# A trunk of attention and feed-forward layers: other banks for two accumulators of the last attention branch, and turns and value products grouped by unit

## Chip, core and metric

The kernel runs on one core of one Trainium2 chip. The metric is the device time of one execution in microseconds (us). It was run three times: median 1346.76 us, lowest 1345.96, highest 1348.61.

## What is computed

Two layers (DEPTH = 2) work on 256 positions of 1024 features. Each layer is a half-weighted SwiGLU feed-forward, an attention block with three branches, a second feed-forward, and a gated projection:

```python
for i in range(DEPTH):
    h = h + 0.5 * swiglu(rms_norm(h, norm_g[i, 0]), ffn1_wi[i], ffn1_wo[i])
    n = rms_norm(h, norm_g[i, 1])
    ... = split_cols(n @ w_in[i], IN_SPLITS)
    ya = diff_attention(...)      # branch a: 4 heads of two score maps
    yb = nsa_attention(...)       # branch b: compressed + selected + window keys, 8 heads in 2 groups
    yc = swa_sink_attention(...)  # branch c: window of 128 and a sink
    merged = (sigmoid(ga) * (ya @ w_branch[i, 0]) + sigmoid(gb) * (yb @ w_branch[i, 1])
              + sigmoid(gc) * (yc @ w_branch[i, 2]))
    h = h + merged @ w_out[i]
    h = h + 0.5 * swiglu(rms_norm(h, norm_g[i, 2]), ffn2_wi[i], ffn2_wo[i])
    h = h + sigmoid(rms_norm(h, norm_g[i, 3]) @ w_ple_gate[i]) * (p[i] @ w_ple[i])
return rms_norm(h, final_norm)
```

All of it is float32. The kernel splits each operand into a high and a low part and forms a product as three matmuls, high times high, high times low, low times high (`mul3`, lines 235 to 237).

## The kernel before

The 256 positions are two tiles, t = 0 and t = 1, of 128. Weights come in pieces of 128x1024 (`raw`), which ScalarE copies to a high part `wh` (line 228) and VectorE subtracts to a low part `wl` (line 223). Six pieces fit (`WBUFS`), so a piece can be written when an older one has been read by both tiles. A product of 8 steps runs tile 0 first and tile 1 eight steps behind it.

Attention work is written as generators that advance by a step after some matmuls of the projections ("`flow.tick`"). A scheduler then orders the instructions of each engine by its own model of their times, so the order in the code is not the order on an engine.

Branch b has six units, called B1 to B6 here: B1 and B2 are tile 0 of key groups 0 and 1 with both key sets, B3 and B4 tile 1 of group 0 with the selected and the window keys, B5 and B6 the same of group 1. `first` of a unit makes the scores (`s`, line 537) and the softmax: VectorE's line 546, ScalarE's exponentials (line 548), and VectorE's scalings of `p`. `second` turns the weights `p` on TensorE four blocks at a time (`pt`, line 243), splits each turn into high and low `pT` (ScalarE line 228, then VectorE line 223; three buffers), and adds two products of 512 columns for each turn to `yb` (`weighted`, lines 790 and 791). Each of B1 to B6 has two turns. After B1, B2, B4 and B6 a compressed part (`own`, `pcT`) is added to `yb`, and `gather` moves `yb` to `yt` (ScalarE lines 796 and 797, VectorE line 800) and splits it to `yB`, which `br` reads.

PSUM (the accumulators that TensorE writes) has eight banks in named rings: `mm` 2, `s` 2, `tp` 3 (all transposes), `y` 1. So B5's first product into `yb` has to wait until `gather` of B4 has read the one `y` bank.

The last branch, b, ends so: both gate products, then `tile(0)`, then `tile(1)`: the two halves (c = 0, 1) of `br` for that tile, each mixed into `merged` by VectorE (lines 970 and 971), transposed (`mt`, line 243) and split to `mT` (lines 231 and 232). Then come the two halves of the product with `w_out` (`wo`). `wo` of tile 0 needs `mT` of tile 0 only; `wo` of tile 1 needs the end of `tile(1)`.

The `product` function takes its banks from `mm`, and where `wide[0]` is set two of every four from `s`:

```python
    def product_bank(name):

        wide[1] += 1
        return bank("s" if wide[0] and wide[1] % 4 >= 2 else "mm", 2, name)
```

Of the kernel before, what the change touches and what calls it, by code (L numbers as in the profile page):

```python
# [186 lines left out]
def trunk(ctx: ExitStack, tc: tile.TileContext, a: dict, out: bass.AP, index: list):  # L187
# [14 lines left out]
    wide = [True, 0]  # L202
# [9 lines left out]
    def y_bank(name):  # L212
        return bank("y", 1, name)
# [290 lines left out]
    def attention(i, norm, after):  # L504
# [76 lines left out]
        qk, va, yA = [None] * 2, [None], [None] * NT  # L581
# [16 lines left out]
        def attend_a():  # L598
            bnd = band(0)

            def first(u):
                m, t = u
                nk = 128 * (t + 1)
                s = scores("s", qk[m], [0, 1], t, lambda x, r, k: qk[m][r, x, 2 + k, :nk])
                yield
                p = pool.tile([128, 4, 256], F32, tag="p", bufs=3, name="p")
                st = None
                for st in softmax([p[:, j, :nk] for j in range(4)], [s[j // 2][:, j % 2, :nk] for j in range(4)],
                                  [back(bnd[:, 2 * m + j % 2], nk) for j in range(4)]):
                    yield  # L610
                nc.vector.reciprocal(st[:, 8:12], st[:, 4:8])
                nc.vector.tensor_scalar(st[:, 10:12], st[:, 10:12], nlam[:, i:i + 1], None, op0=ALU.mult)
                for x in range(2):
                    nc.vector.tensor_scalar(p[:, 2 + x, :nk], p[:, 2 + x, :nk], st[:, 10 + x:11 + x], None, op0=ALU.mult)
                    nc.vector.scalar_tensor_tensor(p[:, x, :nk], p[:, x, :nk], st[:, 8 + x:9 + x], p[:, 2 + x, :nk],
                                                   op0=ALU.mult, op1=ALU.add)
                yield
                return p

            def second(u, p):  # L620
                m, t = u
                T = []
                for k in range(t + 1):
                    T.append(turned([p[:, x, k * 128:(k + 1) * 128] for x in range(2)]))
                    yield
                y_ps = y_bank("ya")[:, :256]
                for x in range(2):
                    o, hd = slice(x * 128, x * 128 + 128), slice((2 * m + x) * 128, (2 * m + x + 1) * 128)
                    for k in range(t + 1):
                        mul3(y_ps[:, o], T[k][:, 0, x, :], T[k][:, 1, x, :], va[0][:, 0, k, hd], va[0][:, 1, k, hd], k == 0, k == t)  # L630
                    yield
                y = pool.tile([128, 256], F32, tag="yt", bufs=2, name="yn")
                st = pool.tile([128, 32], F32, tag="st", bufs=4, name="st")
                for x in range(2):
                    o = slice(x * 128, x * 128 + 128)
                    nc.scalar.activation(y[:, o], y_ps[:, o], AF.Square, accum_out=st[:, x:x + 1])
                nc.vector.tensor_scalar(st[:, 2:4], st[:, 0:2], 1.0 / 128, EPS, op0=ALU.mult, op1=ALU.add)
                nc.gpsimd.tensor_tensor(st[:, 4:6], st[:, 2:4], mhalf[:, :2], op=ALU.pow)
                nc.vector.tensor_tensor(y.rearrange("p (h e) -> p h e", h=2), y_ps.rearrange("p (h e) -> p h e", h=2),
                                        st[:, 4:6, None].to_broadcast([128, 2, 128]), op=ALU.mult)  # L640
                yield
                if m == 0:
                    yA[t] = y_tile("yA")
                ps = tp_bank("yt")
                transposes(ps, [y[:, x * 128:x * 128 + 128] for x in range(2)])
                split(yA[t][:, 0, 2 * m:2 * m + 2], yA[t][:, 1, 2 * m:2 * m + 2],
                      ps[:, :256].rearrange("p (k q) -> p k q", k=2), sg[:, i:i + 1])
                yield

            yield from pipelined([(m, t) for m in range(2) for t in range(NT)], first, second)  # L650


# [189 lines left out]
        def attend_b():  # L842
            bnd, y_ps = {}, {}

            def first(u):
                g, t, ss = u
                if g not in bnd:
                    bnd[g] = band(4 + 4 * g)
                if t == 0:
                    p = pool.tile([128, 4, 2, 128], F32, tag="p", bufs=3, name="p")  # L850
                    s = scores("s", qB[0], [2 * g, 2 * g + 1], 0, lambda x, r, m: kB[0][r, x, g:g + 3:2, :128])
                    rows = [(j, k) for j in range(4) for k in range(2)]
                    pr = [p[:, j, k] for j, k in rows]
                    sr = [s[j // 2].rearrange("p m (k n) -> p m k n", k=2)[:, j % 2, k] for j, k in rows]
                    br = [back(bnd[g][:, j], 128) for j, k in rows]
                else:
                    p = pool.tile([128, 4, 256], F32, tag="p", bufs=3, name="p")
                    s = scores("s", qB[0], [2 * g, 2 * g + 1], 1, lambda x, r, m: kB[0][r, x, 2 * ss[0] + g, :])
                    pr = [p[:, j] for j in range(4)]
                    sr = [s[j // 2][:, j % 2] for j in range(4)]  # L860
                    br = [back(bnd[g][:, j], 256) for j in range(4)]
                n = len(pr)
                yield
                st = None
                for st in softmax(pr, sr, br):
                    yield
                nc.vector.reciprocal(st[:, 2 * n:3 * n], st[:, n:2 * n])
                for k, x in enumerate(ss):
                    o = st[:, 2 * n + k:3 * n:len(ss)]
                    nc.vector.tensor_tensor(o, o, sig[t][:, 8 + 8 * x + 4 * g:12 + 8 * x + 4 * g], op=ALU.mult)  # L870
                for j in range(n):
                    nc.vector.tensor_scalar(pr[j], pr[j], st[:, 2 * n + j:2 * n + j + 1], None, op0=ALU.mult)
                yield
                return p

            def second(u, p):
                g, t, ss = u
                if yB[t] is None:
                    yB[t] = y_tile("yB")
                if ss[0] == 0:  # L880
                    y_ps[g, t] = y_bank("yb")
                for x in ss:
                    for k in range(t + 1):
                        T = turned([p[:, j, x, :] if t == 0 else p[:, j, 128 * k:128 * k + 128] for j in range(4)])
                        yield
                        weighted(y_ps[g, t], vB[0][:, x, k, g], T.rearrange("p x j q -> p x (j q)"), x == 0 and k == 0, False)
                        yield
                if ss[-1] == 1:
                    while t not in pcT:
                        yield  # L890
                    T = own(t, g)
                    yield
                    weighted(y_ps[g, t], vc[0][:, 0], T.rearrange("p x j q -> p x (j q)"), False, True)
                    gather(yB[t], y_ps[g, t], g)
                    readyB[t] += 1
                    yield

            yield from pipelined([(g, t, ss) for t, sets in ((0, [(0, 1)]), (1, [(0,), (1,)])) for g in range(2) for ss in sets], first, second)
# [16 lines left out]
        def attend_c():  # L915
# [26 lines left out]
            def second(u, p):  # L942
                g, t = u
                y_ps = y_bank("yc")
                for k in range(t + 1):
                    T = turned([p[:, j, 128 * k:128 * k + 128] for j in range(4)])
                    yield
                    weighted(y_ps, vC[0][:, k, g], T.rearrange("p x j q -> p x (j q)"), k == 0, k == t)
                    yield
                gather(yC[t], y_ps, g)  # L950
                yield
# [4 lines left out]
        def branch(b, yT, side, last=False):  # L956
# [32 lines left out]
            if last:  # L989
# [3 lines left out]

                def tile(t):
                    for c in range(2):
                        ps = product_bank(f"br{t}")
                        for k in range(4):
                            wh, wl = ws[c](k)
                            mul3(ps, yT[t][:, 0, k, :], yT[t][:, 1, k, :], wh, wl, k == 0, k == 3)
                            flow.tick()  # L1000
                        with tc.high_priority(offset=150):
                            both[c][1](t, ps)
# [40 lines left out]
        yield lambda: start("compressed", compressed(), 1.0, 1)  # L1043
        yield from branch(2, yC, "c")
        yield from branch(1, yB, "b", True)
        yield lambda: wide.__setitem__(0, True)
        for c in range(2):
            yield product(lambda t, k: (mT[t][:, 0, k, :], mT[t][:, 1, k, :]), NK, after(c), "wo", streamed(i, f"wo{c}", 512))

# [197 lines left out]
```

## Time and profile before

| what | value |
|---|---|
| median of 3 runs | 1346.76 us |
| the profiled execution | 1346.13 us, of which the span in the profile is 1344.3 us |
| granted TensorE clock, mean | 0.999 |
| busy: TensorE matmul, weight load, VectorE, ScalarE | 99%, 81%, 70%, 58% |
| attention of layer 0, of layer 1 | about 196 to 462 us, about 860 to 1126 us |

A busy share is that of the whole span. Matmuls overlap in the profile: a row's duration is longer than the distance to the next row's start, and the distance is what a matmul costs.

### The profile page before, as it was taken

What the parts mean: (1) busy time and instruction counts of PE and PEld (TensorE: products, weight loads), DVE (VectorE), ACT (ScalarE), POOL (GpSimd) and SP (SyncE); (2) the same over time, 40 slices, a digit from 0 to 9 for tenths busy, and PEclk for the clock granted to TensorE, in tenths of its full rate; (3) what the DMA queues carried; (4) which work ended last, traced back from release to release, by engine and by line L of the source; (5) the groups of instructions that cost most, each with busy time, mean ns of one, the idle gap of its engine ahead of it and who ended that gap; (6) DMA issues with size and microseconds to landing.
All of it is one profiled execution on the core that took longest, in us unless ns stands there. A gap on an engine that the chain in (4) does not pass through costs nothing.

```text
span 1344.3 us, 18242 instructions
## 1 busy us (share of the span) xinstructions
PE 1326.3 (99%) x6414; PEld 1093.2 (81%) x6414; DVE 945.9 (70%) x1795; ACT 783.0 (58%) x1382; POOL 20.4 (2%) x36
## 2 busy tenths in 40 slices
PE   9999999999999999999999999999999999999997
PEld 7778888887887788888888888888888878888886
DVE  6677566768978767665776766577697886767565
ACT  7555455668756555544755545566696656555454
POOL 0000000000000000000000000000000000000000
PEclk9999999999999999999999999999999999999999
DMA  8887665455742578675567875744556425877562
GB/s 302 214 270 220 206 207 187 141 165 168 229 153 79 188 186 237 208 219 184 188 199 216 224 209 186 243 152 162 167 174 207 152 78 177 242 222 214 189 209 78
DMA packets 121993, 257.14 MB, mean 191 GB/s; under 512 B 56944, under 2 KB 62500, under 8 KB 121902
## 3 DMA queue, kind: packets, MB, share of 16 engines
q1 hardware_dynamic: 121150, 254.34, 61.1%
q0 software_dynamic: 320, 1.08, 0.3%
q8 instruction: 50, 0.82, 0.3%
q10 hardware_dynamic: 432, 0.56, 0.1%
q14 instruction: 41, 0.34, 0.1%
HBM read 243.33 MB, written 1.08 MB: 182 GB/s over the span
## 4 chain that ended last, share of the span: by engine, by line
PE 91%; DVE 4%; DMA 2%; ACT 1%; issue 1%; SPq 0%; POOLq 0%; POOL 0%; DVEq 0%; ACTq 0%
PE ff L236 11%; PE ff L237 11%; PE ff L235 11%; PE fo L235 6%; PE fo L236 6%; PE fo L237 6%; PE gate L235 3%; PE gate L237 3%; PE gate L236 3%; PE s L537 2%; PE A L235 2%; PE A L236 2%; PE A L237 2%; DVE wl L223 2%; PE br L236 1%; PE br L235 1%
## 5 line engine op out<-in xcount | busy, mean ns | idle before, releaser
L223 DVE TENSOR_TENSOR wl<-raw,wh 128x1024 fp32r<-128x1024 f32 (+1 forms) x448 | 539.4, 1213 | 174.2 <-ACT wh L228 166.8
L228 ACT ACTIVATE wh<-raw 128x1024 fp32r<-128x1024 f32 (+1 forms) x448 | 468.3, 1050 | 229.0 <-PE fo L237 85.4
L236 PE MATMUL ff<-wl,nT 128*128 128x512 f32 x704 | 273.8, 391 | 1.6 <-DVE wl L223 1.5
L237 PE MATMUL ff<-wh,nT 128*128 128x512 f32 x704 | 272.8, 390 | 0.0
L235 PE MATMUL ff<-wh,nT 128*128 128x512 f32 x704 | 270.9, 391 | 0.3 <-ACT wh L228 0.3
L236 PEld LDWEIGHTS ff<-wl,nT 128*128 128x128 f32 x704 | 132.3, 188 | 30.9 <-DVE wl L223 3.9
L235 PEld LDWEIGHTS ff<-wh,nT 128*128 128x128 f32 x704 | 132.3, 188 | 29.5 <-ACT wh L228 2.1
L237 PEld LDWEIGHTS ff<-wh,nT 128*128 128x128 f32 x704 | 132.3, 188 | 27.3
L236 PE MATMUL fo<-wl,gT 128*128 128x512 f32 x352 | 134.2, 392 | 0.0
L237 PE MATMUL fo<-wh,gT 128*128 128x512 f32 x352 | 133.7, 389 | 0.0
L235 PE MATMUL fo<-wh,gT 128*128 128x512 f32 x352 | 132.5, 389 | 0.0
L474 ACT ACTIVATE act<-ff,stats 128x256 f32<-128x256 f32 x88 | 41.4, 472 | 85.9 <-PE ff L237 85.7
L475 DVE TENSOR_TENSOR gated<-act,ff 128x256 f32<-128x256 f32 x88 | 36.6, 417 | 60.1 <-ACT act L474 60.1
L235 PEld LDWEIGHTS fo<-wh,gT 128*128 128x128 f32 x352 | 66.1, 188 | 13.8
L237 PEld LDWEIGHTS fo<-wh,gT 128*128 128x128 f32 x352 | 66.1, 188 | 13.4
L236 PEld LDWEIGHTS fo<-wl,gT 128*128 128x128 f32 x352 | 66.1, 188 | 13.3
L235 PE MATMUL gate<-wh,nT 128*128 128x512 f32 x192 | 76.3, 399 | 0.0
L237 PE MATMUL gate<-wh,nT 128*128 128x512 f32 x192 | 76.1, 396 | 0.0
L236 PE MATMUL gate<-wl,nT 128*128 128x512 f32 x192 | 75.9, 395 | 0.0
L228 ACT ACTIVATE gT<-whole 128x512 fp32r<-128x512 f32 (+1 forms) x48 | 28.4, 591 | 64.3 <-DVE whole L448 64.2
L548 ACT ACTIVATE p<-p,st 128x128 f32<-128x128 f32 (+1 forms) x128 | 56.8, 445 | 2.9 <-DVE st L546 2.2
L448 DVE COPY whole<-flip 128x512 uint16<-128x512 uint16 (+1 forms) x96 | 38.2, 433 | 14.5 <-DMA flip<-cut 13.9
(301 smaller groups left out, 1997.6 us busy)
## 6 DMA issues: line engine op xcount, KB each, us to landing
raw<-in_wst SPq DMA_DIRECT2D x438, 512.0 KB, 4.4
band<-table SPq DMA_DIRECT2D x10, 512.0 KB, 5.1
raw<-in_wbv SPq DMA_DIRECT2D x4, 420.0 KB, 3.0
flip<-cut SPq DMA_TRANSPOSE x96, 4.1
xt<-in_xt SPq DMA_DIRECT2D x4, 256.0 KB, 5.3
raw<-in_wst SPq DMA_DIRECT2D x4, 256.0 KB, 4.9
h<-in_x SPq DMA_DIRECT2D x2, 512.0 KB, 7.6
band<-table POOLq DMA_DIRECT2D x2, 512.0 KB, 6.9
```

The lines of the kernel that those rows point to most:

```text
L223: nc.vector.tensor_tensor(o, x, y, op=ALU.subtract)
L228: nc.scalar.activation(hi, src, AF.Copy)
L235: nc.tensor.matmul(ps, xh, wh, start=start, stop=False)
L236: nc.tensor.matmul(ps, xh, wl, start=False, stop=False)
L237: nc.tensor.matmul(ps, xl, wh, start=False, stop=stop)
L448: tc.keep_in_program_order(nc.vector.tensor_copy(halves(whole)[:, :128 * m, w], flip[:, w, :m].rearrange("p a b -> p (a b)")))
L474: nc.scalar.activation(act, ps[:, :256], AF.Silu, scale=norm.r(t))
L475: nc.vector.tensor_tensor(held[t][:, 256 * (f % 2):256 * (f % 2) + 256], act, ps[:, 256:], op=ALU.mult)
L537: nc.tensor.matmul(o, q[r, x, qb[m], t * 128:(t + 1) * 128], kk, start=x + y == 0, stop=x == 1)
L548: nc.scalar.activation(p[j], p[j], AF.Exp, bias=st[:, j:j + 1], scale=-1.0, accum_out=st[:, n + j:n + j + 1])
```

## The change

1. Branch a: a unit's two turns become one run of four transposes with one split of 128x512.
2. Branches b and c: all turns of a unit stand ahead of its value products in the code.
3. `yb` of B5 and B6 is taken from the ring `s`, whose last scores are those of B6.
4. The first half of `tile(1)`'s `br` is taken from `s` too; the other three stay in `mm`.
5. At the end of the branch the counter `wide[1]` is set to -1, so that both tiles of the first `wo` half use `mm` and both of the second `s`.

```diff
-                T = []
-                for k in range(t + 1):
-                    T.append(turned([p[:, x, k * 128:(k + 1) * 128] for x in range(2)]))
-                    yield
+                T = turned([p[:, x, k * 128:(k + 1) * 128] for k in range(t + 1) for x in range(2)])
+                yield
...
-                    y_ps[g, t] = y_bank("yb")
-                for x in ss:
-                    for k in range(t + 1):
-                        T = turned([p[:, j, x, :] if t == 0 else p[:, j, 128 * k:128 * k + 128] for j in range(4)])
-                        yield
-                        weighted(y_ps[g, t], vB[0][:, x, k, g], T.rearrange("p x j q -> p x (j q)"), x == 0 and k == 0, False)
-                        yield
+                    y_ps[g, t] = bank("s", 2, "yb") if g == t == 1 else y_bank("yb")
+                parts = [(x, k) for x in ss for k in range(t + 1)]
+                T = [turned([p[:, j, x, :] if t == 0 else p[:, j, 128 * k:128 * k + 128] for j in range(4)]) for x, k in parts]
+                yield
+                yield
+                for (x, k), turns in zip(parts, T):
+                    weighted(y_ps[g, t], vB[0][:, x, k, g], turns.rearrange("p x j q -> p x (j q)"), x == 0 and k == 0, False)
+                    yield
...
+                T = [turned([p[:, j, 128 * k:128 * k + 128] for j in range(4)]) for k in range(t + 1)]
+                for _ in T:
+                    yield
                 for k in range(t + 1):
-                    T = turned([p[:, j, 128 * k:128 * k + 128] for j in range(4)])
-                    yield
-                    weighted(y_ps, vC[0][:, k, g], T.rearrange("p x j q -> p x (j q)"), k == 0, k == t)
+                    weighted(y_ps, vC[0][:, k, g], T[k].rearrange("p x j q -> p x (j q)"), k == 0, k == t)
                     yield
...
-                        ps = product_bank(f"br{t}")
+                        ps = bank("mm" if t == 0 or c else "s", 2, f"br{t}")
...
-        yield lambda: wide.__setitem__(0, True)
+        yield lambda: wide.__setitem__(slice(0, 2), [True, -1])
```

The order changes on all engines from the second half of branch a on, and is the same in both layers. Three places follow, all in layer 0; numbers behind a name tell tiles apart.

TensorE of before, where B4's `yb` ends and B5's begins (`yb_3833` is B4's, `yb_4083` B5's and B6's, `pt_4137` and `pt_4156` are B6's two turns, `mt_4219` turns the first half of tile 0's `merged`):

```order
L790 MATMUL yb_3833<-pcT_3999,vc_3514 128x512
L243 MATMUL pt_4137<-ident_66,p_4017 128x128 x4
L791 MATMUL yb_3833<-pcT_3999,vc_3514 128x512
L243 MATMUL pt_4156<-ident_66,p_4017 128x128 x4
L243 MATMUL mt_4219<-ident_66,merged0_1722 128x128 x4
L790 MATMUL yb_4083<-pT_4089,vB_2572 128x512
L791 MATMUL yb_4083<-pT_4089,vB_2572 128x512
```

TensorE of the change at the same place (`yb_3815` is B4's, `yb_4075` B5's and B6's, `pt_4126` and `pt_4134` are B6's turns, `mt_4211` and `mt_4245` those of tile 0's `merged`):

```order
L788 MATMUL yb_3815<-pcT_3988,vc_3506 128x512
L788 MATMUL yb_4075<-pT_4081,vB_2569 128x512
L243 MATMUL pt_4126<-ident_66,p_4009 128x128 x4
L789 MATMUL yb_3815<-pcT_3988,vc_3506 128x512
L789 MATMUL yb_4075<-pT_4081,vB_2569 128x512
L243 MATMUL pt_4134<-ident_66,p_4009 128x128 x4
L788 MATMUL yb_4075<-pT_4089,vB_2569 128x512
L243 MATMUL mt_4211<-ident_66,merged0_1722 128x128 x4
L789 MATMUL yb_4075<-pT_4089,vB_2569 128x512
L788 MATMUL yb_4075<-pT_4131,vB_2569 128x512
L243 MATMUL mt_4245<-ident_66,merged0_1722 128x128 x4
```

B5's first value products stand among B4's last ones and B6's turns, ahead of both `mt`, and B6's two turns are still apart.

VectorE at that place, before (`th` and `merged0` mix tile 0; `pT_4120` is B5's second turn, `pT_4142` and `pT_4161` are B6's):

```order
L970 SCALAR_TENSOR_TENSOR th_3975<-th_3975,br0_4182 128x512
L970 SCALAR_TENSOR_TENSOR th_4126<-th_4126,br0_4226 128x512
L971 TENSOR_TENSOR merged0_1722<-merged0_1722,th_3975 128x512
L223 TENSOR_TENSOR pT_4120<-pt_4115,pT_4120 128x512
L971 TENSOR_TENSOR merged0_1722<-merged0_1722,th_4126 128x512
L800 TENSOR_TENSOR yt_4007<-yt_4007,yb_3833 64x256 x2
L223 TENSOR_TENSOR pT_4142<-pt_4137,pT_4142 128x512
L232 SCALAR_TENSOR_TENSOR mT_4218<-mt_4219,mT_4218 128x512
```

VectorE of the change (`pT_4089` is B5's second turn, `pT_4131` and `pT_4139` are B6's):

```order
L970 SCALAR_TENSOR_TENSOR th_3975<-th_3975,br0_4183 128x512
L971 TENSOR_TENSOR merged0_1722<-merged0_1722,th_3975 128x512
L970 SCALAR_TENSOR_TENSOR th_4118<-th_4118,br0_4218 128x512
L223 TENSOR_TENSOR pT_4089<-pt_4084,pT_4089 128x512
L971 TENSOR_TENSOR merged0_1722<-merged0_1722,th_4118 128x512
L798 TENSOR_TENSOR yt_3999<-yt_3999,yb_3815 64x256 x2
L223 TENSOR_TENSOR pT_4131<-pt_4126,pT_4131 128x512
L223 TENSOR_TENSOR pT_4139<-pt_4134,pT_4139 128x512
L232 SCALAR_TENSOR_TENSOR mT_4210<-mt_4211,mT_4210 128x512
```

The operations are the same; the first `merged` half moved up by one place, and B6's second `pT` from behind `mT` to ahead of it.

TensorE at the end of `tile(1)`, before (`br1` is the last half of tile 1, `mt_4276` turns the first half of its `merged`, `wo1_4371` is `wo` of tile 1):

```order
L237 MATMUL br1_4283<-wh_4205,yB_3832 128x512
L235 MATMUL br1_4283<-wh_4205,yB_3832 128x512
L236 MATMUL br1_4283<-wl_4206,yB_3832 128x512
L237 MATMUL br1_4283<-wh_4205,yB_3832 128x512
L243 MATMUL mt_4276<-ident_66,merged1_1723 128x128 x4
L235 MATMUL wo1_4371<-wh_4228,mT_4275 128x512
```

And of the change (`wo0_4303` and `wo0_4411` are the two `wo` halves of tile 0, `mt_4268` and `wo1_4363` as above):

```order
L237 MATMUL br1_4275<-wh_4197,yB_3814 128x512
L236 MATMUL wo0_4303<-wl_4312,mT_4210 128x512
L237 MATMUL wo0_4303<-wh_4311,mT_4210 128x512
L235 MATMUL wo0_4303<-wh_4311,mT_4210 128x512
L236 MATMUL wo0_4303<-wl_4312,mT_4210 128x512
L237 MATMUL wo0_4303<-wh_4311,mT_4210 128x512
L235 MATMUL wo0_4411<-wh_4323,mT_4210 128x512
L243 MATMUL mt_4268<-ident_66,merged1_1723 128x128 x4
L235 MATMUL wo1_4363<-wh_4220,mT_4267 128x512
```

Six matmuls of tile 0's `wo` now stand between the last `br` and the turn of `merged`.

## Rows read from the trace of the kernel before

**Rows 1.** The page: busy time of each engine, share of the span.

```profile
PE 1326.3 (99%) x6414; PEld 1093.2 (81%) x6414; DVE 945.9 (70%) x1795; ACT 783.0 (58%) x1382; POOL 20.4 (2%) x36
```

**Rows 2.** TensorE's waits, both layers: us in total, times, longest.

```profile
PE yb L790 <- DVE yt L800: 1.9, 4, 0.8
PE wo L235 <- ACT mT L231: 1.6, 2, 0.8
...
PE mt L243 <- DVE merged L971: 1.4, 2, 0.7
```

**Rows 3.** Window from B6's scores to `wo`: PE, PEld, DVE, ACT, POOL busy; clock; DMA.

```profile
416.69:444.84 28.15, 24.93 (x121) 19.48 (x119) 21.70 (x47) 15.78 (x33) 0.00 (x0) 1.00 0.20 65
```

**Rows 4.** Timeline of TensorE there: start, duration, what, [idle before <-releaser].

```profile
415.15 0.38 PE L537 MATMUL s<-kB,qB 64*128 64x256 f32 x2
415.47 0.50 PE L791 MATMUL yb<-pcT,vc 128*128 128x512 f32 x1
415.90 0.86 PE L537 MATMUL s<-kB,qB 64*128 64x256 f32 x10
416.69 0.50 PE L237 MATMUL br<-wh,yB 128*128 128x512 f32 x1
...
424.97 0.60 PE L243 MATMUL pt<-ident,p 128*128 128x128 f32 x4
425.32 0.48 PE L791 MATMUL yb<-pcT,vc 128*128 128x512 f32 x1
425.64 0.60 PE L243 MATMUL pt<-ident,p 128*128 128x128 f32 x4
426.46 0.66 PE L243 MATMUL mt<-ident,merged 128*128 128x128 f32 x4 [0.22 <-DVE pT L223]
427.91 0.47 PE L790 MATMUL yb<-pT,vB 128*128 128x512 f32 x1 [0.80 <-DVE yt L800]
...
437.23 0.50 PE L236 MATMUL wo<-wl,mT 128*128 128x512 f32 x1 [0.57 <-DVE wl L223]
...
438.73 0.39 PE L235 MATMUL br<-wh,yB 128*128 128x512 f32 x1
...
441.22 0.39 PE L236 MATMUL br<-wl,yB 128*128 128x512 f32 x1
...
443.43 0.63 PE L243 MATMUL mt<-ident,merged 128*128 128x128 f32 x4 [0.69 <-DVE merged L971]
444.84 0.50 PE L235 MATMUL wo<-wh,mT 128*128 128x512 f32 x1 [0.78 <-ACT mT L231]
```

**Rows 5.** Timeline of VectorE there.

```profile
421.68 1.13 DVE L872 TENSOR_SCALAR p<-p,st 128x256 f32<-128x256 f32 x4
...
423.93 1.27 DVE L970 SCALAR_TENSOR_TENSOR th<-th,br 128x512 f32<-128x512 f32 x2
...
426.92 0.84 DVE L800 TENSOR_TENSOR yt<-yt,yb 64x256 f32<-64x256 f32 x2
...
435.95 1.22 DVE L223 TENSOR_TENSOR wl<-raw,wh 128x1024 fp32r<-128x1024 f32 x1 [3.46 <-ACT wh L228]
```

**Rows 6.** Timeline of ScalarE there.

```profile
413.77 1.04 ACT L228 ACTIVATE wh<-raw 128x1024 fp32r<-128x1024 f32 x1
...
418.03 0.51 ACT L548 ACTIVATE p<-p,st 128x256 f32<-128x256 f32 x1 [0.64 <-DVE st L546]
...
424.94 0.60 ACT L228 ACTIVATE pT<-pt 128x512 fp32r<-128x512 f32 x1 [2.16 <-PE yb L791]
```

**Rows 7.** Groups by form, 200 to 460 us: splits of turns, busy us, mean ns.

```profile
L223 DVE TENSOR_TENSOR pT<-pt,pT 128x512 fp32r<-128x512 f32 x18 | 12.0, 685 | 0.1
L228 ACT ACTIVATE pT<-pt 128x512 fp32r<-128x512 f32 x18 | 10.2, 588 | 4.5 <-PE yb L791 3.3 <-PE pt L243 1.2
...
L223 DVE TENSOR_TENSOR pT<-pt,pT 128x256 fp32r<-128x256 f32 x6 | 2.4, 417 | 3.2 <-ACT pT L228 3.2
L228 ACT ACTIVATE pT<-pt 128x256 fp32r<-128x256 f32 x6 | 2.2, 385 | 4.1 <-PE pt L243 4.1
```

More of the change, by code (lines that the diff above doesn't have):

```diff
@@ L629, in second @@
                     for k in range(t + 1):
-                        mul3(y_ps[:, o], T[k][:, 0, x, :], T[k][:, 1, x, :], va[0][:, 0, k, hd], va[0][:, 1, k, hd], k == 0, k == t)
+                        mul3(y_ps[:, o], T[:, 0, 2 * k + x, :], T[:, 1, 2 * k + x, :], va[0][:, 0, k, hd], va[0][:, 1, k, hd], k == 0, k == t)
                     yield
```

## The prediction

> **What bounds the kernel now.** I read the page's busy times first: the matmuls of TensorE are busy for 99% of the span [rows 1], so a change pays only where TensorE stands still. The list of TensorE's waits is short, and within attention every wait lies in the last 30 us: the same list asked for 190 to 416 us is empty, so no row stands for it. Per layer the longest entries are `yb` waiting for `yt` (1.9 us in four waits over two layers), `wo` for `mT`, `mt` for `merged` [rows 2]; the timeline adds `wo` for `wl` (0.57) and `mt` for `pT` (0.22) [rows 4]. The window of that stretch, from the end of B6's scores to the first `wo` of tile 1, lasts 28.15 us, and VectorE is busy for 21.70 of it, ScalarE for 15.78 [rows 3]. The reader should see there a TensorE that has run out of work that is ready, behind VectorE's queue.
>
> **The stretch in pure work.** Eleven matmuls of 512 columns lie between the starts 438.73 and 441.22, so one costs 0.227. Four transposes hold TensorE 0.35, and the matmul behind them takes 0.32 to the next start, some 0.09 more: 0.44 a run [rows 4]. By the order, the stretch holds 87 matmuls of 512 columns and 8 fours: 19.75 + 3.5 = 23.25. So 4.9 of the 28.15 are lost, the waits themselves 3.2 of it, the rest in refilling. That is the most that can be won: 9.8 us over both layers. The other layer has the same waits [rows 2].
>
> **The change, part by part.**
>
> *One run per unit in branch a.* Two units per layer replace two ScalarE splits of 385 ns by one of 588, and two VectorE splits of 417 by one of 685 [rows 7]: 0.33 us of engine time saved per unit. The first value product comes up to 0.2 + 0.27 = 0.47 later, as it now waits for the whole split; four such units make 1.9 us at most. I take nothing: projections stand beside it on TensorE and no wait is listed there; if that cover were gone it would cost the 1.9. The Trainium skill, Perfetto Trace Analysis, section "Optimizing Scalar/DVE Operations", speaks against this edit: where these engines aren't saturated but make others wait, smaller instructions may finish work sooner. By that rule the sum would lose up to those 1.9 us; the trace has no such wait to act on.
>
> *Turns ahead of products in branches b and c.* No instruction is added. By the order, runs of transposes per layer rise from 41 to 48 and runs of score matmuls fall from 27 to 23. A run of transposes costs 0.09 extra, so 0.6. Ten score matmuls take 0.79 and two alone 0.32 [rows 4], 0.16 over their share, so four fewer runs give back 0.6. I take zero, with 0.6 per layer either way as bounds.
>
> *Banks.* B5's products no longer wait for the `gather` of B4: waits of 0.95 us per layer go [rows 2], and their refill, 0.3 or so. What is late next needs the whole order, because VectorE loses no work. I place the new order on the durations of the rows, per layer, with zero at the end of B6's scores.
>
> The new order leaves more behind the scores: 8 gate and 24 `br` matmuls of tile 0, against 19 `br`; 14 matmuls more in the whole stretch (one is a `wo`). So the same work would have lasted 28.15 + 14 x 0.227 = 31.3 before.
>
> - ScalarE is free for it at about 1.0 and has, in order, `wh`, `yB`, two exponentials of B6, `th`, `wh`, two exponentials: 1.0 + 0.4 + 1.0 + 0.6 + 1.0 + 1.0 (a 128x512 at 0.55 to 0.6) [rows 6, 7]. B6's exponentials are done at 6.0.
> - VectorE: small ones 0.35, a `pT` 0.6, four scalings 1.1 [rows 5]: 8.1. Then `pcT` and `pT` to 9.3, `th` and `merged` of the first half to 10.5, `th` of the second to 11.1 (two `th` take 1.27).
> - TensorE, meanwhile: 38 matmuls and three turns, 8.6 + 1.3 = 9.95. It does not wait: B6's turns come at 10.9, 2.8 after the scalings.
> - B5's second turn needs one of three `pT` buffers, free when TensorE has made two more products, 10.4. ScalarE splits it by 11.05, VectorE by 11.7, then `merged` 12.3, the `yt` pair 13.15, B6's two `pT` 13.75 and 14.35.
> - TensorE from 9.95: seven matmuls and two turns, 12.4; first `mt` 12.85; two products 13.3. The second `mt` needs the `tp` bank that VectorE reads until 13.75: 0.45 lost. Done 14.2; then 4 products, 4 `br`, 12 `wo`, the last product, 8 `br`: 29 matmuls, 20.8.
> - The third piece of `wo`'s weights needs a buffer that `br` of tile 1 frees at 19.85. ScalarE copies it by 20.95, behind the `gather`; TensorE waits 0.25. VectorE's `wl` is 1.2 [rows 5], ready at 22.1; the matmuls that need it come at 22.2.
> - 25 more matmuls (`wo`, `br`) end at 26.7. `merged` of tile 1 is ready at 25.7, since six `wo` now stand ahead of `mt`: the 0.69 goes. From `mt` to `wo` of tile 1 it is 444.84 - 443.43 = 1.41 as before [rows 4]: 28.1.
>
> I add 0.5 for some five hand-overs between engines that the walk puts at nothing: 28.6. Gain 31.3 - 28.6 = 2.7 per layer. Bounds: 4.9, if all that is lost comes back, and below zero by the last rival.
>
> *The counter.* The first `wo` half now takes both `mm` banks. Tile 0's is read by `th` at 11.1, five us ahead of its first `wo`; tile 1's by `th` of tile 1 at about 26.5, ahead of 28.1. Nothing; uncovered, a late `th` would cost its 0.6.
>
> **Sum.** 2 x 2.7 = 5.4 from the profiled 1346.13 (span 1344.3 and 1.8 around it) is 1340.7. The median of the runs is 0.63 above that execution, so I say 1341.4.
>
> **Rivals.**
>
> 1. *Only the named wait goes.* `yb` for `yt` is 1.9 us over both layers [rows 2]; the waits for `wl`, `merged` and `mT` stay, as they follow from VectorE's queue. That gives 1344.9 at the median. For it: four of the five kinds of wait don't hang on this bank. Against: the order puts six more independent `wo` ahead of tile 1's `mt`, and 14 matmuls more behind the scores.
>
> 2. *The wait moves.* VectorE keeps all its work, and the `tp` banks, three as before, are freed by VectorE in order; TensorE then waits at `mt` for what it waited at `yb`. The walk shows this at 0.45; if VectorE is 2.7 later than there, the gain is used up: 1346.8. The Trainium skill, TensorE: Matmul & The Clock Gate, section "HAM oscillation — how this bites in real kernels", reports that PSUM double-buffering gave one kernel no further gain. By that rule the time stays; the trace neither shows nor excludes it.
>
> 3. *Slower: ScalarE stands at a `pT` buffer.* A unit's two turns now follow each other on ScalarE, and the second of B5 waits for a product that stands behind 16 `br`. Such waits exist (2.16 us at 424.94 [rows 6], 3.3 in all [rows 7]), and the queue behind it is the `gather` copies, B6's splits, `mT`, `pcT` and `yB`: from 10.4 to 15.0 everything that TensorE needs passes through it in turn. TensorE's cover from 10.4 is 13 matmuls and four runs, 4.7. If that cover went ahead of the wait, 4.7 more would be lost per layer, net 2.0 worse: 1350.8. It decides from 2.7 uncovered on; over 0.2% slower needs 4.1. Against it: the order interleaves that cover.
>
> 4. *The change doesn't do what it says.* In part so: B6's turns stay apart in the new order. The banks are taken as the code says.
>
> **Chances.** 0.2% is 2.7 us, about what a measurement of this kernel can tell. The forecast, a gain of 2.8 to 8: 0.67, its own range 1338.5 to 1344. Rival 1: 0.15, and rival 2: 0.10, both within 0.2%. Rival 3: 0.08, slower by over 0.2% in most of it. So faster 0.67, same 0.26, slower 0.07. The range runs from 1338.0, near the bound of 9.8, to 1346.3, which takes in rival 1 and leaves out rival 3 and half of rival 2.
>
> **What would show it.** In the profile after: no TensorE wait of `yb` for `yt`; `mt` of tile 1 without a wait for `merged`; a wait of some 0.5 at tile 0's second `mt` for `pT`, a short one at the third piece of `wo`, and `wo` for `mT` still near 0.8 per layer; the stretch from the end of B6's scores to tile 1's `wo` at 28 to 29 us; no wait in 190 to 410. I am wrong if `mt` or `yb` of the first tile wait over 1.5 us, if ScalarE's wait before B5's second `pT` is followed by TensorE's own, or if waits appear in branches a and c.

## The result

The change runs in 1340.03 us (median of 6 runs, 1339.4 to 1341.89) against 1346.59 for the kernel before (6 runs): ratio 0.9948, interval 0.9937 to 0.9959, 6.6 us faster. The forecast was 1341.4.

The page of the changed kernel, busy times as in [rows 1]:

```profile
PE 1322.5 (99%) x6414; PEld 1091.2 (82%) x6414; DVE 948.1 (71%) x1791; ACT 778.7 (58%) x1378; POOL 18.6 (1%) x36
```

TensorE is again busy for 99%, but for 3.8 us less, with the same 6414 instructions. TensorE's waits, to be read beside [rows 2]:

```profile
PE wo L235 <- ACT mT L231: 1.4, 2, 0.7
PE mt L243 <- DVE pT L223: 1.2, 2, 0.6
...
PE ya L235 <- ACT pT L228: 0.5, 1, 0.5
PE gl L739 <- DVE c_sb L732: 0.5, 2, 0.3
PE wo L235 <- ACT wh L228: 0.5, 2, 0.2
```

`yb` no longer waits for `yt`, nor `mt` for `merged`, nor `wo` for `wl`. Two small waits in the earlier branches are new (`ya`, `gl`). The timeline of the stretch, as in [rows 4]:

```profile
413.98 0.50 PE L236 MATMUL gate<-wl,nT 128*128 128x512 f32 x1
...
426.65 0.60 PE L243 MATMUL mt<-ident,merged 128*128 128x128 f32 x4
...
428.46 0.63 PE L243 MATMUL mt<-ident,merged 128*128 128x128 f32 x4 [0.57 <-DVE pT L223]
...
435.97 0.50 PE L235 MATMUL wo<-wh,mT 128*128 128x512 f32 x1 [0.24 <-ACT wh L228]
...
441.91 0.60 PE L243 MATMUL mt<-ident,merged 128*128 128x128 f32 x4
443.20 0.50 PE L235 MATMUL wo<-wh,mT 128*128 128x512 f32 x1 [0.69 <-ACT mT L231]
```

The stretch lasts 29.22 (28.15 in [rows 3] with 14 matmuls fewer, so 31.3 for the same work): 2.1 gained per layer.

Attention has to be looked at as a whole, though. The windows view from the first `A` matmul (branch a's projection) to the first `ff` matmul (the feed-forward behind attention), per layer: length, busy time of TensorE (first number) and of the other engines. The last two lines are the same windows for instructions on the score tile `s` alone. Before:

```profile
191.75:462.58 270.83, 267.61 (x1443) 220.44 (x1442) 207.54 (x478) 179.56 (x384) 3.33 (x5) 1.00 0.51 168
855.15:1125.94 270.79, 267.56 (x1443) 220.45 (x1442) 207.36 (x478) 179.44 (x384) 3.33 (x5) 1.00 0.52 168
191.75:462.58 270.83, 19.10 (x168) 14.05 (x168) 20.06 (x64) 1.00 0.51 168
855.15:1125.94 270.79, 19.10 (x168) 14.05 (x168) 20.05 (x64) 1.00 0.52 168
```

After:

```profile
192.38:460.77 268.39, 266.12 (x1444) 219.55 (x1442) 208.20 (x475) 176.55 (x383) 3.33 (x5) 1.00 0.52 170
853.25:1120.24 266.99, 265.23 (x1443) 219.56 (x1442) 208.09 (x475) 176.92 (x381) 3.32 (x5) 1.00 0.53 171
192.38:460.77 268.39, 17.51 (x168) 13.32 (x168) 20.08 (x64) 1.00 0.52 170
853.25:1120.24 266.99, 17.12 (x168) 13.28 (x168) 20.08 (x64) 1.00 0.53 171
```

Attention is 2.44 shorter in layer 0 and 3.80 in layer 1, 6.2 of the 6.6. Length less busy time is what TensorE stood idle: 3.22 before in both layers, 2.27 and 1.76 after. So only 0.95 + 1.47 = 2.4 of the 6.2 is waiting. The larger part, 1.49 + 2.33 = 3.8, is busy time, and the 168 score matmuls account for nearly all of it: 1.59 + 1.98 = 3.6 for the same matmuls. TensorE has the same work and does it faster.

One correction of what stands ahead of the prediction: the new order is not the same in both layers. By the names in the trace, the layers differ among matmuls 171 to 471 of attention's 1442 (228 to 275 us in layer 0). So there are 23 runs of score matmuls in layer 0 and 21 in layer 1; a run is a row of them with no other matmul between. Of the 1.36 that layer 1 gains more, 0.39 is busy time of scores, 0.45 other busy time, and 0.51 the wait of `ya`, which layer 0 alone has.

Executions also differ by up to 4 us in when attention begins (its first matmul at 190.8 to 195.0 us in these profiles), ahead of everything that the edits touch (what goes with it stands in the last section). Beside the medians the lengths of attention are therefore compared; those repeat to 0.1.

### The profile page after: what moved, and what is told of

Its sections match the earlier page's. It is cut to its first block, busy times and chain, and to the rows that moved or that the text cites. A ratio compares the mean times of both kernels' runs of the same rounds, so it can differ in the third digit from the quotient of the medians.

```text
span 1338.5 us, 18237 instructions
## 1 busy us (share of the span) xinstructions
PE 1322.5 (99%) x6414; PEld 1091.2 (82%) x6414; DVE 948.1 (71%) x1791; ACT 778.7 (58%) x1378; POOL 18.6 (1%) x36
## 4 chain that ended last, share of the span: by engine, by line
PE 91%; DMA 3%; DVE 3%; ACT 1%; issue 1%; SPq 0%; POOLq 0%; POOL 0%; DVEq 0%; ACTq 0%
PE ff L236 11%; PE ff L235 11%; PE ff L237 11%; PE fo L235 6%; PE fo L236 6%; PE fo L237 6%; PE gate L235 3%; PE gate L237 3%; PE gate L236 3%; PE s L537 2%; PE A L236 2%; PE A L235 2%; PE A L237 2%; PE br L235 2%; PE br L236 2%; PE br L237 1%
```

## The experiments

Theory 1 is that of the prediction: the banks make the gain, edit 1 next to nothing in the stretch. Theory 2: edit 1 makes it, by what it does to the order. Theory 3: both are needed together. Later expectations name their theories A, B and C, each for itself.

**1. Edit 1 alone.**

```diff
-                T = []
-                for k in range(t + 1):
-                    T.append(turned([p[:, x, k * 128:(k + 1) * 128] for x in range(2)]))
-                    yield
+                T = turned([p[:, x, k * 128:(k + 1) * 128] for k in range(t + 1) for x in range(2)])
+                yield
```

> Edit 1 alone (one run of turns per unit in branch a); banks and branches b and c as before. By the order it already has the 14 more matmuls behind B6's scores and 23/21 runs of scores per layer for 27. Theory 1 (the banks made the gain of the stretch, 2.1 per layer; edit 1 only the 2.1 of both layers ahead of it): 1344.5, y's wait of 0.8 to 0.95 per layer still there, the stretch some 31 us. Theory 2 (edit 1 made it all, by its order): 1340 to 1341.5, the stretch at 29.2 to 30 in spite of y's wait. Theory 3 (cover and bank are worth something only together): 1344 to 1345, and the banks alone no more than 0.5 faster than before.

Measured 1343.02, ratio 0.9968 (0.9956 to 0.998). The windows of attention, and those of the scores alone:

```profile
192.02:462.10 270.08, 266.40 (x1443) 219.54 (x1442) 208.70 (x476) 177.60 (x382) 3.32 (x5) 1.00 0.51 169
854.68:1123.30 268.62, 265.44 (x1444) 219.50 (x1442) 208.65 (x476) 178.01 (x382) 3.32 (x5) 1.00 0.51 169
192.02:462.10 270.08, 17.51 (x168) 13.33 (x168) 20.11 (x64) 1.00 0.51 169
```

Busy time falls by 1.2 and 2.1; the idle time is 3.7 and 3.2, for 3.2 before. The gain is 0.75 and 2.17 per layer, and it isn't waits.

**2. Edits 3, 4 and 5 alone.**

```diff
-                    y_ps[g, t] = y_bank("yb")
+                    y_ps[g, t] = bank("s", 2, "yb") if g == t == 1 else y_bank("yb")
...
-                        ps = product_bank(f"br{t}")
+                        ps = bank("mm" if t == 0 or c else "s", 2, f"br{t}")
...
-        yield lambda: wide.__setitem__(0, True)
+        yield lambda: wide.__setitem__(slice(0, 2), [True, -1])
```

> Edits 3, 4 and 5 alone (banks and counter), branch a as before. Theory 1: 1342.5, 4.2 faster than before, all of it in the stretch, no wait of yb for yt. Theory 2: 1346 to 1347, the wait moved to mt, the stretch as long as before for its work. Theory 3: within 0.5 of before, as theory 2, but edit 1 alone doesn't give the whole gain either.

Measured 1342.51, ratio 0.9967 (0.9955 to 0.9979):

```profile
195.00:464.22 269.22, 267.54 (x1443) 220.44 (x1442) 206.92 (x478) 178.84 (x385) 3.33 (x5) 1.00 0.51 169
```

Here the busy time is that of before and the idle time halves, 3.22 to 1.68: 1.6 per layer. With experiment 1 the gains add: 0.75 + 1.61 = 2.36 in layer 0 (2.44 measured together), 2.17 + 1.57 = 3.74 in layer 1 (3.80). All three theories fail as put: each edit does its part by itself, at its own place.

**3. Edit 2 alone** (the turns ahead of the products in branches b and c, as in the change's diff).

> Edit 2 alone (turns of branches b and c ahead of their products in the code). The order of each engine comes out the same as before, row for row. So all theories say 1346.6, within the spread of the runs of before: this run is also the measure of what no change looks like. If it differs by over 1 us, something beside the order counts (addresses of buffers, DMA order).

Measured 1346.26, ratio 0.9998 (0.9989 to 1.0006), attention 270.83 and 270.85. Edit 2 does nothing: the scheduler makes the same program of it. Nor does it add to edit 1: by the names in the traces, TensorE's matmuls in experiment 1 and in the change come in one order for the first 1279 of attention's 1442, in both layers, and differ only behind them, where the last `yb` products moved. The shift in runs that the prediction put down to it comes from edit 1.

**4. The change without edits 4 and 5** (`br` and the counter as before).

> The change without edits 4 and 5: B5's and B6's yb from the ring of the scores, but tile 1's br from the banks as before. Theory 1 with the y bank as what counts: 1340 to 1341, as the whole change. If br's bank counts: 1342 or more, with a wait of br1 for th or of mt for merged in the stretch of 0.7 per layer. Theory 2: as edit 1 alone.

Measured 1339.87, attention 268.40 and 266.98, as the whole change. In the stretch `wo` waits 0.47 for `pT` in place of `mt`'s 0.57.

**5 and 6. Edit 3 alone; edits 4 and 5 alone** (the first hunk of experiment 2's diff; its other two).

> Edit 3 alone: yb of B5 and B6 from the ring of the scores. The three edits on banks together took 1.6 per layer out of the stretch. If the y bank is the whole of that: attention 269.2 per layer, 1342.5 to 1343. If br's bank is needed for it (rival): the wait of mt for merged or of wo for wl stays, 0.6 to 0.7 per layer, attention 269.9, 1344.

> Edits 4 and 5 alone: tile 1's first br from the ring of the scores, and the counter. Theory: nothing, attention 270.8 per layer, 1346 to 1347, with all waits of before. Rival (br's bank carries part of the gain): 0.5 or more per layer faster, 1345 to 1346.

Measured 1342.25 (0.9965, 0.9953 to 0.9978), attention 269.16: edit 3 is all that the banks give. Edits 4 and 5 alone: 1346.75 (1.0004, 0.9995 to 1.0013), attention 270.6 (0.2 less), with the waits of before, but 0.5 less for `wo` over both layers.

From here on theory A: edit 1 pays by how the scheduler places the score matmuls. Its rows are in the timeline of TensorE before, where branch c's last unit and B2 make their 12 scores each:

```profile
310.88 0.50 PE L537 MATMUL s<-kC,qC 64*128 64x256 f32 x2
311.31 0.49 PE L790 MATMUL yc<-pT,vC 128*128 128x512 f32 x1
311.74 0.74 PE L537 MATMUL s<-kC,qC 64*128 64x256 f32 x4
312.40 0.50 PE L235 MATMUL gate<-wh,nT 128*128 128x512 f32 x1
...
313.06 0.62 PE L537 MATMUL s<-kC,qC 64*128 64x256 f32 x3
313.61 0.50 PE L791 MATMUL yc<-pT,vC 128*128 128x512 f32 x1
314.05 0.62 PE L537 MATMUL s<-kC,qC 64*128 64x256 f32 x3
314.59 0.50 PE L237 MATMUL gate<-wh,nT 128*128 128x512 f32 x1
...
338.19 0.98 PE L537 MATMUL s<-kB,qB 64*128 64x256 f32 x6
339.09 0.33 PE L730 MATMUL cmp<-wh,es 128*64 128x256 f32 x1
339.35 0.97 PE L537 MATMUL s<-kB,qB 64*128 64x256 f32 x6
340.25 0.33 PE L731 MATMUL cmp<-wl,es 128*64 128x256 f32 x1
```

After, the same two units:

```profile
312.16 0.97 PE L537 MATMUL s<-kC,qC 64*128 64x256 f32 x6
313.06 0.50 PE L789 MATMUL yc<-pT,vC 128*128 128x512 f32 x1
313.49 0.98 PE L537 MATMUL s<-kC,qC 64*128 64x256 f32 x6
314.40 0.50 PE L237 MATMUL gate<-wh,nT 128*128 128x512 f32 x1
...
336.46 0.98 PE L537 MATMUL s<-kB,qB 64*128 64x256 f32 x12
337.37 0.33 PE L728 MATMUL cmp<-wh,es 128*64 128x256 f32 x1
```

From a run's first start to the next row's start: 0.43 + 0.66 + 0.55 + 0.54 = 2.18 becomes 0.90 + 0.91 = 1.81, and 0.90 + 0.90 = 1.80 becomes 0.91. Two things cost here. A run has a price of its own: two scores take 0.32 and ten 0.79 [rows 4], so 0.059 for each score and 0.20 for the run. Its neighbours of 512 columns pay too: the run starts 0.32 after the matmul ahead of it began, instead of 0.227, and the matmul behind it takes 0.34 to the next start. And the order within a run counts: a score uses rows 0 to 63 or 64 to 127 of its operands; by the order of the engine B2's two sixes before use one half each (0.90 a six), its twelve after alternate (0.91 a twelve). B1, in three pieces before (0.31 + 0.79 + 0.32), takes 0.91 after.

The Trainium skill, TensorEngine Tiling (Array Packing), sections "Available Configurations" and "Key Properties", states both: operands of 64 rows put TensorE into another tiling mode, a change of mode drains it, and different tiles can work in parallel. The trace agrees in what it can show: 0.20 and some 0.2 on the neighbours for a run, and 0.90 for six scores on one half against 0.55 for six that alternate. That a drain is what the run pays for, no run here shows. Nor do the runs tell the half from the accumulator bank: the scores of each half go to a bank of their own, so neighbours on one half are also neighbours in one bank.

**7 and 8. Edit 1 in halves**: one split but as many steps; two splits but one step less.

```diff
-                T = []
+                T = turned([p[:, x, k * 128:(k + 1) * 128] for k in range(t + 1) for x in range(2)])
                 for k in range(t + 1):
-                    T.append(turned([p[:, x, k * 128:(k + 1) * 128] for x in range(2)]))
                     yield
```

```diff
                     T.append(turned([p[:, x, k * 128:(k + 1) * 128] for x in range(2)]))
-                    yield
+                yield
```

> Half of edit 1: one run of four turns and one split per unit of branch a, but with as many steps as before. By the order 43 runs of turns and 29 of scores per layer (before 41 and 27, edit 1 whole 46/48 and 23/21), and the 14 more matmuls behind B6's scores. Theory A (edit 1 pays by fewer runs of scores, some 0.35 each): no gain from it ahead of the stretch, 0.5 to 1 slower there per layer than before, 1347 to 1348.5 in all, or as before if the stretch gives back 0.5. Theory B (it pays by the smaller splits on VectorE and ScalarE): 1343 to 1344, as edit 1 whole.

> The other half of edit 1: two runs of two turns and two splits as before, but one step fewer per unit of branch a. By the order 45/46 runs of turns and 29/23 of scores in layers 0 and 1 (before 41 and 27). Theory A (runs of scores, some 0.35 each, turns 0.09): layer 0 slower by 1, layer 1 faster by 0.9, so 1346 to 1347.5 in all. Theory B (splits): as before in both layers, within 0.5.

One split: 1346.72 (1.0002, 0.9993 to 1.0011), attention 271.1, the scores busy for 19.92. It has all the saving of the splits and gains nothing, so theory B falls. Of theory A the second outcome came, as before: the scores cost 0.82 more, and the stretch gives back 0.5 (30.56, as in experiment 1). One step less: 1351.27 (1.003, 1.0018 to 1.0042). Layer 1, with 23 runs, came to 271.05 and not below 270.8: the scores are busy 0.7 less, but TensorE idles 0.8 more. Layer 0 came to 275.94: scores 1.7 more, and new waits (1.57 at B6's turns) with what follows them (last section). Theory A had the sign of layer 0 alone, not its size (5.1 slower for 1); what was saved in layer 1 went into waits. Neither half gives what edit 1 gives.

**9. The kernel before, with its scores alone rearranged.**

```diff
-                    for par in range(2):
+                    for par in (1, 0):
...
-                        nc.tensor.matmul(o, q[r, x, qb[m], t * 128:(t + 1) * 128], kk, start=x + y == 0, stop=x == 1)
+                        with tc.high_priority(offset=1000 if m or x or y or par != 1 else 0):
+                            mm = nc.tensor.matmul(o, q[r, x, qb[m], t * 128:(t + 1) * 128], kk, start=x + y == 0, stop=x == 1)
+                        if m or x or y or par != 1:
+                            tc.keep_in_program_order(mm)
```

> The kernel before with one thing changed: the 12 score matmuls of a unit are kept in one chain that alternates between the two banks (rows 64 to 127 and 0 to 63 of the operands), and are preferred by the scheduler. By the order 21 runs of scores per layer for 27, no two neighbours on the same half (before 57 per layer), 42 runs of turns for 41, 105 matmuls behind B6's scores for 87. Theory A (runs of scores and same-half neighbours are what edit 1 pays by): a run costs 0.20 + 0.059 for each score inside and 0.21 on the matmuls beside it, so 21 x 0.41 + 168 x 0.059 = 18.5 per layer for the 23.6 that the trace of before shows: 5.1 per layer faster, 1336 to 1338. Theory B (edit 1 pays by more matmuls behind B6's scores, by cover): as edit 1 alone, 1342.5 to 1344. Theory C (by its splits): 1346 to 1347.

Measured 1339.69, ratio 0.9949 (0.9935 to 0.9962), 7.3 faster, with none of the change's edits:

```profile
191.21:458.43 267.22, 263.95 (x1444) 217.61 (x1442) 208.75 (x478) 177.96 (x384) 3.33 (x5) 1.00 0.51 171
191.21:458.43 267.22, 15.96 (x168) 11.95 (x168) 20.08 (x64) 1.00 0.51 171
```

All of it is busy time (3.66 less, the scores 3.14 of it); the idle time is as before, 3.27, so cover (theory B here) gave nothing. Theory A holds in kind; its 5.1 per layer came to 3.65.

**10. The same edit on the change.**

> The change with the same edit of the scores. By the order 20 runs of scores per layer (for 23 and 21), no same-half neighbours (for 60), 46/49 runs of turns for 48/50. Theory A: 20 x 0.41 + 168 x 0.059 = 18.1 per layer for the 21.0 and 20.5 of the change, so 5.3 faster in all: 1334.5 to 1336. Theories B and C: within 1 of the change, 1339 to 1341. If the new order makes waits in the stretch (TensorE's list shows them), they are taken off first.

Measured 1341.15 (0.995, 0.9938 to 0.9963), attention 268.45 and 266.84: nothing gained over the change. The scores did get cheaper, 15.78 busy for 17.51 and 17.12, but the list of TensorE's waits shows where it went:

```profile
PE gate L236 <- DVE wl L223: 2.1, 2, 1.0
```

Gate products moved up to where their weights weren't split yet, and idle time rose to 3.7 and 2.7. The expectation (1334.5 to 1336) failed: it had allowed for new waits in the stretch, and these came ahead of it, the one in layer 0 at 346 us.

**11. The scores' edit and edit 3, nothing else.**

> The scores in alternating chains (as in the run on the kernel before: attention 267.15 per layer) and edit 3, the y bank (1.6 per layer by itself); no edit of branch a. By the order 21 runs of scores, 44 of turns per layer. Theory: the two gains add, since they are taken at different places: attention 265.5 per layer, 1336 to 1337, 3 to 4 faster than the change. Rival (as with the change and the scores together, where new waits took it): 1339 to 1340, with new waits of TensorE ahead of B6's scores.

Measured 1336.07, ratio 0.9922 (0.9909 to 0.9934):

```profile
192.15:457.77 265.62, 263.93 (x1444) 217.69 (x1442) 208.34 (x478) 177.28 (x385) 3.33 (x5) 1.00 0.52 172
```

Busy time as in experiment 9, idle time 1.69 as with the banks: the gains add. It is 10.5 faster than before; the change's ratio to before is 0.9948.

**12. As experiment 9, but six scores of one half and then six of the other** (the loop over `par` outside those over `m`, `x` and `y`).

> As the scores in chains on the kernel before, but a unit's six scores of one half first and then its six of the other. By the order 19 runs of scores per layer (alternating: 21) and 140 neighbours on the same half (0). It tells the two parts of theory A apart. If the number of runs is what counts: attention 266.5 per layer, 1338 to 1339. If same-half neighbours cost 0.034 each (12 scores take 1.25 so and 0.91 alternating): 140 x 0.034 = 4.8 more than the alternating chains, less 0.8 for two runs: attention 271, 1346 to 1348.

Measured 1351.92, ratio 1.0038 (1.0024 to 1.0052). A unit's twelve scores in the timeline, and the scores' window:

```profile
414.29 1.32 PE L538 MATMUL s<-kB,qB 64*128 64x256 f32 x12
415.54 0.50 PE L794 MATMUL yb<-pT,vB 128*128 128x512 f32 x1
...
193.52:467.18 273.66, 20.93 (x168) 17.42 (x168) 20.33 (x64) 1.00 0.50 166
```

Two runs fewer than in experiment 9 and yet 5.0 us more of busy scores per layer: twelve scores take 1.25 in halves and 0.91 alternating. So the order inside the runs counts for far more here than two runs fewer. Of the 6.4 by which attention is longer than in experiment 9, 1.0 is new waiting. The second theory's 271 and 1346 to 1348 were passed by 2.7 and 4: besides the waiting, the 0.8 that it took off for two runs fewer doesn't show, so the 0.41 for a run with its neighbours was probably too high. No run prices it by itself.

## Why the prediction was right, and where its steps were not

The time was within 1.4 us and in the range, but that close by luck, through two errors of opposite sign: 5.4 was forecast from the banks and 0 from edit 1, and by themselves they took 3.2 (1.61 + 1.57) and 2.9 (0.75 + 2.17) from attention.

- **"A change pays only where TensorE stands still."** This sentence failed first. TensorE's busy share of 99% hid 19.1 us of scores per layer that the order alone can make 16.0, or 20.9.
- **Edit 1 taken at nothing.** The bound of 1.9 lost was right in kind: `ya`, the first value product, waits 0.5, in layer 0 alone. The wait of `gl` (a product of branch b's compressed keys), 0.26 per layer, the prediction did not have. "No wait in 190 to 410" was therefore wrong, and one of its own signs of being wrong, waits in branches a and c, came true with `ya`. What was missing is the order of the scores, which the prediction met under edit 2 and sized at 0.16 for each run saved, to cancel against 0.09 for each run of turns. Measured, the scores' busy time fell by 1.59 and 1.98, and everything else that TensorE does changed by +0.10 and -0.35, so the seven to nine more runs of turns cost nothing that shows. The 0.16 left out what a run costs the matmuls beside it, and the halves altogether. Counting runs was the right idea; +-0.6 was too narrow a bound.
- **Edit 2.** It changes nothing in the program (experiment 3), so its bounds were never in play.
- **Banks: 2.7 per layer.** Right in kind, 1.6 in size. The waits went as the walk had them: 0.57 at tile 0's second `mt` (0.45 forecast), 0.24 at the third piece of `wo`'s weights (0.25), `merged` gone, `mT` 0.69 (0.8). The stretch, 29.2, is 0.6 above the 28.6 of the walk, and 0.56 of the 2.1 gained there came with edit 1: by itself it takes the stretch to 30.54 with 13 more matmuls, where 28.15 + 13 x 0.227 is 31.10. The mis-sized term is the refilling. The work of the stretch is 101 x 0.227 + 3.5 = 26.4; 28.6 left 0.7 beside 1.5 of waits, and measured are 1.3 beside 1.5. What was lost there without being idle was not to be won by a bank: the banks alone leave the busy time where it was.
- **The counter and `br`'s bank at nothing.** Right to within 0.2 per layer (experiments 4 and 6).
- **Rivals.** The first (only the named wait, 1.9) fell short: the banks alone took 3.2 from attention, as the waits for `merged` and `wl` went too. Of the second, 0.57 per layer did move to `mt`. In the third ScalarE did stand before B5's second `pT`, for 3.71 (at 424.80), and TensorE lost no more than the 0.57; its cover held. The fourth was true of edit 2.

## What to carry to other kernels

A busy engine is not an engine at its best: compare the busy time of one tile's instructions between two orders before taking 99% as the bound. Where a scheduler orders the work, a small edit far from the costly place can pay or cost by how it packs matmuls of another shape; count runs, look at what alternates inside them, and price both from the timeline. An edit that is cheap by itself should be tried apart: here one of the three edits on banks and one of the two on turns did nearly all the work, and the packing, done on purpose, was worth as much as both together (ratio 0.9949 for 0.9948).

## What the runs showed of the hardware

- Scores of 64 rows and 256 columns that alternate between the two halves take 0.059 each, beside the run's own 0.20. A six on one half alone takes 0.90, so 0.117 each; two such sixes in one run 1.25, 0.09 each. Three and three cost nothing: in the change's runs at 394.2 and 395.2 us a six in the order `aaabbb` (by the order of the engine) and an alternating six take 0.55 each.
- A stand of TensorE can cost twice. In experiment 8 it was busy for 1.25 of 3 us (the 1.57 wait), and the granted clock was 0.54 in the next 3 us, so mostly at the lower of its two levels, 1.2 GHz for 2.4. The windows view there, with busy times and the clock behind them:

```profile
431.00:434.00 3.00, 1.25 (x10) 0.79 (x9) 2.92 (x7) 1.94 (x5) 0.00 (x0) 1.00 0.00 0
434.00:437.00 3.00, 2.98 (x8) 2.22 (x9) 2.21 (x4) 0.92 (x2) 0.00 (x0) 0.54 0.03 5
```

Eight matmuls ran in those 3 us, 0.43 apart for 0.23. No wait of the change or of the kernel before had this behind it: their clock in attention is 1.00.
- The same fall goes with a late start of attention. Near 67 us the first feed-forward waits for a `wl`, for longer in some executions than in others. Experiment 2 waited 2.31 there and the change 1.68; from 70 to 73 us one had the lower level and the other kept the higher:

```profile
70.00:73.00 3.00, 3.00 (x9) 2.26 (x8) 2.98 (x4) 1.37 (x3) 0.00 (x0) 0.50 0.84 250
70.00:73.00 3.00, 3.00 (x15) 2.45 (x14) 2.94 (x7) 1.71 (x3) 0.00 (x0) 1.00 0.85 240
```

Nine matmuls ran for fifteen. The five profiles with such a fall near 70 us (experiments 2, 6, 8, 10 and 12) are the five whose attention begins at 193.5 us or later.
